# First chunk from turned tokens with late rates, and the last output columns kept in PSUM: a hybrid encoder layer on one Trainium2 core

## The chip, the cores and the metric

The kernel runs on one core of a Trainium2 chip. The metric is the device time of one execution in microseconds (us). The engines are PE (TensorE: products and transposes), DVE (VectorE), ACT (ScalarE), POOL (GpSimd) and SP (SyncE, which here only issues DMAs). PE writes into PSUM, eight banks of 512 float32 per partition; the others read it from there, POOL apart.

## The reference

One layer over 2048 tokens and 16 meta tokens ahead of them, 1024 channels, float32:

```python
u = rms_norm(h, pre_g)
proj = u @ w_in            # 1024 x 3584
glu_a, glu_b, conv_gate, q, k, v, sb_gate = split(proj)   # 512 columns each
c = glu_a * sigmoid(glu_b)
c = causal_depthwise_conv(c, conv_w, conv_b)              # width 31
c = silu(layer_norm(c, conv_ln_g, conv_ln_b))
c = (c @ w_pw2 + b_pw2) * silu(conv_gate)
s = stick_breaking_attention(heads(q), heads(k), heads(v)) * silu(sb_gate)  # 8 heads x 64
mixed = concatenate([c, s]) @ w_out                       # 1024 x 1024
return h + rms_norm(mixed, post_g)                        # meta tokens dropped
```

`rms_norm` divides a token's row by the root of its mean square (that factor is called its rate here) and multiplies by a gain per channel.

## The kernel before

Tokens are worked in four chunks of 512 (`TC`), each as four blocks of 128. A float32 product is made of three products of rounded parts: every operand is split into a high part (ACT rounds it) and a low part (DVE or POOL subtracts). So `uh` and `ul`, the two parts of the normed tokens, stand with channels on the partitions, eight pieces of 128 channels (`k`), with 16 + 512 columns; a group of 128 output columns of `w_in` takes 8 x 3 products of up to 512 columns (`mm3`, L571). In chunk 0, with the meta tokens, a group has two halves of 264 columns (`segs`, L593), 48 products in all. Weights come in slabs of 512 columns: the first time raw from `wpack` (two slabs a load, `load_raw`, L512, two buffers), split by ACT and POOL into four buffers `w`, and saved to `wscr` by POOL's queue if they are used again; later both parts come back from `wscr` in one load of 512 KB. `release` (L555) frees a slab and asks for the next.

The start: `load_in` (L631) loads the 512 tokens of chunk 0 as rows, `norm_in` (L641) squares them on ACT, makes the rate on POOL and scales them on DVE; `turn_in` (L659) turns them on PE, 32 transposes of 128 x 128, and ACT and DVE make `uh` and `ul` from PSUM with the gain `preg`. The meta tokens take the same way (`meta_norm`, `meta_in`). `in_proj` (L741) then runs the groups of chunk 0: G_B and G_A in turn for the four pieces `j` (sigmoid at the evacuation of G_B, product with it at that of G_A, into `ct`), then K, V and Q. The convolution of a piece is 31 taps on DVE over `ct[j]`, summing in the PSUM bank `cv`; its taps fill gaps of DVE.

Attention of a chunk runs per head and chunk of keys: scores on PE into a bank "T", sigmoid on ACT, a scan on DVE, transposes on PE, split on ACT and DVE, products with v into the bank "av". Products of the projections and of the output run between as filler, by a planner: `merge` (L1554) asks each stream when its next piece can start and keeps two streams in the proportion of `SHARES`; `when` and `in_us` put off steps (loads, splits) to the time at which the planner's clock thinks them ready. The instructions of each engine are in a fixed order once that is done. PSUM has two banks "mm", four "T", one "av", one "cv". SBUF tiles are rings by name: `ev` (six), `w` (four), `wr` (two), `pr` (nine).

The end: for the last chunk `out_part` (L1350) makes the output products of seven of the eight k in four steps of 256 columns (n). Three of them are copied from PSUM to `y` by ACT; the last one stays in two "mm" banks. Its second half is run to two pairs of k ahead (`AHEAD`), the rest in `out_last` (L1382), which then takes the four blocks of 128 tokens one after the other: the products of the last k, additions to `y`, squares on ACT, the product with `post_g` on POOL and DVE, the rate, and output = x + rate * y in two halves, each stored by SP.

In the trace nearly all instructions carry line 204, that of the helper which issues them, so rows are told apart by their tiles.

## Time and profile before

| | us |
|---|---|
| median of 3 runs (lowest to highest) | 1373.24 (1370.44 to 1373.45) |
| the profiled execution | 1371.76 |
| its span, first to last instruction | 1370.0 |
| PE busy in the span | 1312.5 (96%) |
| PE weight loads, beside the products | 1125.2 (82%) |
| DVE busy | 1006.8 (73%) |
| ACT busy | 732.0 (53%) |
| POOL busy | 657.0 (48%) |
| mean granted TensorE clock | 0.992 of full |

The engines work side by side, so their busy times don't add up. The profiled execution's time holds the span and 1.76 us around it. A product's duration in the timeline holds its way through the array, so a run of them is read by start to start, or by a group's span over its count.

### The profile page before, as it was taken

The numbers are of one execution on the slowest core, as the hardware profiler recorded it, in microseconds if no ns is written. First come the engines' busy times: TensorE is split into PE (matmuls) and PEld (weight loads), VectorE is DVE, ScalarE is ACT, GpSimd is POOL, SyncE is SP. The second block draws the span as 40 slices with busy tenths as digits, with TensorE's granted clock in tenths as the row PEclk, the third lists the DMA queues.
The fourth block names the chain that finished last, engine by engine and source line by source line (L and its number), as shares of the span: only waits on it lengthen the run. The fifth ranks groups of instructions, "written<-read, shape, count | busy, mean of one in ns | idle before, by whom it ended". The sixth has DMA issues, their size and how long they took to land. (4 is left out here: it accounts for less than half of the span.)

```text
span 1370.0 us, 21785 instructions
## 1 busy us (share of the span) xinstructions
PE 1312.5 (96%) x7599; PEld 1125.2 (82%) x7599; DVE 1006.8 (73%) x1402; ACT 732.0 (53%) x1452; POOL 657.0 (48%) x794
## 2 busy tenths in 40 slices
PE   6999988999998999999999999999999999999895
PEld 5998877887788977887789988888777898888794
DVE  3999663998984467984495477885549988898666
ACT  5233554444446544476655456578676576655443
POOL 5445486668356631387831243278786111222303
PEclk9999999999999999999999999999999999999998
DMA  4266978999975994686866696567677456587431
GB/s 142 94 164 197 345 233 248 302 316 320 348 245 179 319 339 145 202 236 204 264 223 185 191 326 198 173 190 235 201 220 241 147 173 174 173 276 237 159 109 62
DMA packets 160157, 299.12 MB, mean 218 GB/s; under 512 B 15392, under 2 KB 69344, under 8 KB 160048
## 3 DMA queue, kind: packets, MB, share of 16 engines
q1 hardware_dynamic: 145744, 247.65, 58.9%
q0 software_dynamic: 14304, 50.08, 9.4%
q8 instruction: 60, 0.98, 0.3%
q14 instruction: 49, 0.40, 0.1%
HBM read 216.02 MB, written 81.66 MB: 217 GB/s over the span
## 5 line engine op out<-in xcount | busy, mean ns | idle before, releaser
L204 PE MATMUL mm<-uh,w 128*128 128x512 f32 (+1 forms) x1728 | 522.9, 367 | 2.6 <-POOL w L204 1.5
L204 PEld LDWEIGHTS mm<-uh,w 128*128 128x128 f32 x1728 | 307.6, 188 | 51.5 <-POOL w L204 2.5
L204 DVE TENSOR_TENSOR al<-T,ah 128x512 fp32r<-128x512 f32 (+3 forms) x323 | 194.4, 602 | 168.9 <-ACT ah L204 167.9
L204 PE MATMUL mm<-ul,w 128*128 128x512 f32 (+1 forms) x864 | 312.0, 361 | 0.0
L204 DVE TENSOR_TENSOR_SCAN pr<-T,pr,zcol 128x512 f32<-128x512 f32 x192 | 245.1, 1277 | 55.5 <-ACT T L204 51.4
L204 ACT ACTIVATE ah<-T 128x512 fp32r<-128x512 f32 (+3 forms) x323 | 171.7, 532 | 164.7 <-PE T L204 159.5
L204 DVE SCALAR_TENSOR_TENSOR cv<-ct,cp,cv 128x512 f32<-128x512 f32 x319 | 239.4, 751 | 7.5
L204 ACT ACTIVATE T<-T 128x512 f32<-128x512 f32 (+2 forms) x320 | 167.6, 525 | 96.6 <-PE T L204 92.7
L204 POOL TENSOR_TENSOR acc<-acc,pd 128x512 f32<-128x512 f32 x150 | 193.8, 1292 | 50.6 <-ACT pd L204 43.7
L204 PE MATMUL T<-kk,q 128*128 128x512 f32 (+2 forms) x640 | 195.3, 388 | 2.9 <-DVE pr L204 1.7
L204 POOL TENSOR_TENSOR w<-wr,w 128x512 fp32r<-128x512 f32 x116 | 149.7, 1296 | 98.5 <-ACT w L204 95.2
L204 PE MATMUL T<-ident,pr 128*128 128x128 f32 x1088 | 173.2, 275 | 9.8 <-DVE al L204 6.5
L204 PEld LDWEIGHTS mm<-ul,w 128*128 128x128 f32 x864 | 162.7, 188 | 20.3 <-DVE ul L204 0.2
L204 PEld LDWEIGHTS T<-ident,pr 128*128 128x128 f32 x1088 | 134.1, 141 | 42.3 <-DVE al L204 8.2
L204 DVE TENSOR_TENSOR_SCAN pr<-T,tri 128x128 f32<-128x128 f32 (+3 forms) x128 | 103.8, 815 | 43.0 <-ACT T L204 42.5
L204 ACT ACTIVATE w<-wr 128x512 fp32r<-128x512 f32 x116 | 72.3, 628 | 104.8 <-DMA wr<-wpack 34.9
L204 PEld LDWEIGHTS T<-kk,q 128*128 128x128 f32 x640 | 106.1, 190 | 19.1 <-DVE pr L204 2.8
L204 PE MATMUL av<-ah,vk 128*128 128x512 f32 (+1 forms) x320 | 117.0, 366 | 1.4 <-ACT ev L204 1.4
L204 PE MATMUL av<-al,vk 128*128 128x512 f32 (+1 forms) x320 | 117.4, 367 | 0.0
L204 PE MATMUL mm<-uh,wr 128*128 128x512 f32 x320 | 115.0, 401 | 0.0
L204 ACT ACTIVATE pd<-ct,cp 128x512 f32<-128x512 f32 x150 | 105.9, 717 | 15.3 <-POOL acc L204 14.7
L204 POOL COPY cm<-pr 128x1 f32<-128x1 f32 x120 | 23.3, 206 | 153.4 <-DVE pr L204 153.2
(154 smaller groups left out, 1768.3 us busy)
## 6 DMA issues: line engine op xcount, KB each, us to landing
w<-wscr SPq DMA_DIRECT2D x125, 512.0 KB, 4.2
wscr<-w POOLq DMA_DIRECT2D x76, 512.0 KB, 5.8
wr<-wscr SPq DMA_DIRECT2D x59, 512.0 KB, 4.3
wr<-wpack SPq DMA_DIRECT2D x58, 512.0 KB, 5.2
kk<-kscr SPq DMA_DIRECT2D x80, 256.0 KB, 5.2
vk<-vscr SPq DMA_DIRECT2D x80, 256.0 KB, 4.1
q<-qscr SPq DMA_DIRECT2D x64, 256.0 KB, 6.8
tok<-x SPq DMA_DIRECT2D x16, 512.0 KB, 7.6
```

The source lines that it names most:

```text
L204: return call(out, *args, **kw)
```

## The change

The host gives a second copy of the first chunk with channels first (`xturn`: 16 meta tokens and 512 tokens). The kernel loads it in eight pieces, makes `uh` and `ul` straight from them with the gain but without the rates, and runs the first four groups (G_B and G_A of j = 0 and 1) on that. The token rows are loaded too, behind the turned pieces; their squares give the rates, which five transposes spread over the partitions into `row`. The evacuations of the four groups wait for `row`: G_B's sum is multiplied by it before the sigmoid, and the sigmoid once more after it, so that G_A's sum needs no product of its own. The turned pieces are then scaled and `uh` and `ul` are made again for the groups that follow. The first group does both its halves k by k; the second and third go into "T" banks. Twenty transposes of the identity stand ahead of everything on PE. The `ev` ring goes from six to five tiles. Raw weights are asked for one load at a time, when the planner thinks a buffer free. In `merge`, put-off steps that are ready sooner run first when no stream is ready; some bookkeeping of the planner is finer.

At the end the last 512 output columns instead of the last 256 stay in PSUM, in the banks "cv", "mm", "mm" and "T"; their weights are loaded once for each half of the tokens. The second half's products but two pairs of k are left to `out_last`. There the work is ordered anew: first 512 columns on DVE from "T" banks, last 512 straight from PSUM, the product with `post_g` and all outputs on DVE.

The diff, cut to its core:

```diff
-EV, WB, RAWS, PR, EHL = 6, 4, 2, 9, 4
+EV, WB, RAWS, PR, EHL = 5, 4, 2, 9, 4
-    [(29.8, 172.7)], [(73.1, 217.8)], [(116.0, 217.8)], [(125.1, 97.4), (160.4, 136.0)],
+    [(29.8, 172.7)], [(73.1, 217.8)], [(116.0, 217.8)], [(125.1, 97.4), (160.4, 126.3)],
...
+            else:
+                for n in (*range(0, D, OC), *range(D // 2, D, OC)):
+                    yield w_out, n, OC, 0, KD - 1
...
-                    in_us(2.0, load_raw)
+                    when(
+                        lambda: load_raw(min(RAWS, len(raws) + 1)), [], date=pe.now + 2.0, tag="wr")
...
+    def load_first_in():
+        uh, ul = u_now
+        load_raw(1)
+        sp.dma_start(cp, cpack)
+        keep["turned", 0] = 0
+        ts = []
+        for k in range(KD):
+            ts.append(T("pr", [P, TC], PR))
+            sp.dma_start(ts[k], xturn[:, k, NM:])
+            when(lambda k=k: part_in(0, k, ts[k], uh, ul), [ts[k], cp])
+            if k == 0:
+                mt = T("pr", [P, KD, NM], PR)
+                sp.dma_start(mt, xturn[:, :, :NM])
...
+        load_raw()
+        todo = []
+        for i in range(NTB // 2):
+            t = tok()
+            for b in range(2):
+                tb = 2 * i + b
+                sp.dma_start(t[:, b], x[tb * P : (tb + 1) * P, :])
+                todo.append((t[:, b], tb))
...
+        def spread():
+            pt = PT("cv", [P, TC])
+            for tb in range(NTB):
+                pe.transpose(
+                    pt[:, tb * P : (tb + 1) * P], rate0[:, tb : tb + 1].to_broadcast([P, P]),
+                    ident,
+                )
...
+            act.activation(row[:, NM:], pt, AF.Copy)
...
+            for go in waiting:
+                go()
+            for k in range(KD):
+                when(lambda k=k: times(k, pt), [ts[k], pt], [ts[k]])
...
+        def again():
+            yield need(given=lambda: len(scaled) == KD and "first" in keep)
+            keep["turned", 0] = 0
+            keep["normed"] = True
+            meta_in()
+            for k in range(KD):
+                when(lambda k=k: part_in(0, k, ts[k], uh, ul), [ts[k]])
+        return again()
+
+    def warm():
+        pt = PT("T", [P, TC])
+        for _ in range(20):
+            pe.transpose(pt[:, :P], ident, ident)
...
+        first = G_B, G_A, G_B + 1, G_A + 1
+        if c == 0 and g == first[-1]:
+            yield need(given=lambda: "row" in keep)
+        if c == 0 and g not in first:
+            keep["first"] = True
+            yield need(given=lambda: "normed" in keep)
...
+                def go():
+                    dve.tensor_tensor(t, pt, row[:, o : o + n], op=ALU.mult)
+                    act.activation(t, t, AF.Sigmoid)
+                    if j < 2:
+                        pool.tensor_tensor(t, t, row[:, o : o + n], op=ALU.mult)
+                if c == 0 and j < 2:
+                    with_rates(go)
...
+        def late(i, tags):
+            for e in range(2):
+                w = weights(w_out, D // 2 + e * OC, OC, 0, KD - 1)
+                keep["o", i, e] = yield from out_products(
+                    w, mix, range(KD - 1), i, False, tag=tags[e], free=True
+                )
+        yield from late(0, ("cv", "mm"))
+        keep["rest"] = late(1, ("mm", "T"))
...
+        def add_first(tb, a):
+            yt = y[tb // 2][:, tb % 2, 0:TC]
+            dve.tensor_tensor(yt, yt, a, op=ALU.add)
+            square(tb, yt, 0)
+            dve.tensor_tensor(yt, yt, pg[:, 0], op=ALU.mult)
+        def add_second(tb):
+            yt = y[tb // 2][:, tb % 2, TC:]
+            for e in range(2):
+                o, cols = keep["o", tb // 2, e][:, tb % 2], slice(e * OC, (e + 1) * OC)
+                square(tb, o, 1 + e)
+                dve.tensor_tensor(yt[:, cols], o, pg[:, 1, cols], op=ALU.mult)
...
+        rest = keep["rest"]
+        for _ in range(3):
+            next(rest)
+        a = [first(0)]
+        second(0)
+        a += [first(tb) for tb in range(1, NTB)]
+        add_first(0, a[0])
+        finish_off(rest)
+        second(1)
+        add_second(0)
+        add_first(1, a[1])
+        rate(0)
+        add_second(1)
+        add_first(2, a[2])
+        rate(1)
+        give_out(0)
+        add_first(3, a[3])
+        give_out(1)
+        add_second(2)
+        rate(2)
+        add_second(3)
+        rate(3)
+        give_out(2)
+        give_out(3)
...
-        load_in(0, 0)
-        load_in(0, 1)
-        m = load_meta()
-        load_raw()
+        warm()
+        once_more = load_first_in()
+        prepare()
         clear()
...
-        spent = [merge(iter(()), either(in_proj(0), either(turn_in(0), meta_in(m))), iter(()), [(1, 1)])]
+        spent = [merge(iter(()), either(in_proj(0), once_more), iter(()), [(1, 1)])]
...
+        "xturn": np.ascontiguousarray(
+            np.concatenate([f["meta_tokens"], f["x"][0, :TC]])
+            .reshape(NM + TC, KD, P).transpose(2, 1, 0)
+        ),
```

## Rows read from the trace of the kernel before

**Rows 1.** windows, four stretches; columns: busy us (instructions) per engine, granted clock, DMA share, GB/s:

```profile
0.00:42.90 42.90, 30.81 (x231) 28.83 (x232) 20.92 (x32) 21.09 (x36) 21.19 (x39) 1.00 0.43 138
42.90:1342.00 1299.10, 1270.03 (x7287) 1085.55 (x7287) 966.14 (x1333) 702.22 (x1386) 625.42 (x746) 1.00 0.71 224
1342.00:1353.70 11.70, 11.64 (x85) 10.81 (x83) 7.22 (x18) 4.72 (x17) 2.39 (x3) 1.00 0.01 1
1353.70:1370.00 16.30, 0.00 (x0) 0.00 (x0) 12.55 (x21) 3.94 (x14) 7.99 (x8) 0.60 0.34 129
```

**Rows 2.** waits of PE, first 60 us: us in total, times, longest:

```profile
PE T L204 <- DVE tok L204: 11.1, 4, 7.3
```

**Rows 3.** timeline of the start: start us, us, engine, operation, idle before and its releaser:

```profile
9.59 1.06 ACT L204 ACTIVATE ev<-tok 128x1024 bf16<-128x1024 f32 x1 [0.83 <-DMA tok<-x]
...
12.49 2.64 PEld L204 LDWEIGHTS T<-ident,tok 128*128 128x128 f32 x13 [1.80 <-DVE tok L204]
...
18.50 0.86 PEld L204 LDWEIGHTS T<-ident,tok 128*128 128x128 f32 x8 [0.24 <-DVE ul L204]
...
19.36 0.37 PE L204 MATMUL mm<-uh,w 128*128 128x264 f32 x1
...
19.60 2.72 DVE L204 SCALAR_TENSOR_TENSOR ul<-T,cp,uh 128x512 fp32r<-128x512 f32 x4 [0.19 <-ACT uh L204]
```

**Rows 4.** timeline of DVE, 26 to 235 us:

```profile
31.74 0.43 DVE L204 TENSOR_TENSOR ct<-mm,ehl 128x264 f32<-128x264 f32 x1 [2.48 <-PE mm L204]
...
43.42 0.43 DVE L204 TENSOR_TENSOR ct<-mm,ehl 128x264 f32<-128x264 f32 x1
...
143.25 0.75 DVE L204 SCALAR_TENSOR_TENSOR acc<-ct,cp,cv 128x512 f32<-128x512 f32 x1
```

**Rows 5.** DMA queues, 0 to 40 us: GB/s in slices of 1 us:

```profile
GB/s 0 25 266 373 410 389 406 354 276 388 350 51 0 0 0 0 0 20 211 287 70 348 113 0 16 0 0 0 0 123 350 51 0 0 29 264 231 0 0 16
```

**Rows 6.** DMA queues, 102 to 106 us, around the loads of km:

```profile
DMA packets 1660, 0.65 MB, mean 162 GB/s; under 512 B 1143, under 2 KB 1624, under 8 KB 1659
```

**Rows 7.** timeline of the end:

```profile
1341.71 0.39 PE L204 MATMUL av<-al,vk 128*128 128x512 f32 x1
...
1342.64 3.04 PE L204 MATMUL mm<-w,mixc 128*128 128x256 f32 x24
...
1345.53 2.32 PE L204 MATMUL mm<-w,mixs 128*128 128x256 f32 x18
1345.89 0.43 DVE L204 TENSOR_TENSOR mixs<-uh,mixs 128x256 fp32r<-128x256 f32 x1 [0.54 <-ACT mixs L204]
...
1352.31 0.63 ACT L204 ACTIVATE ev<-tok 128x512 bf16<-128x512 f32 x1 [1.16 <-DVE tok L204]
...
1352.33 1.32 PE L204 MATMUL T<-acc,mixs 128*128 128x512 f32 x6
...
1364.23 2.73 DVE L204 SCALAR_TENSOR_TENSOR ul<-tok,st,ul 128x512 f32<-128x512 f32 x4
```

**Rows 8.** groups by shape, 1342 to 1370 us: busy us, mean ns, idle before:

```profile
L204 DVE TENSOR_TENSOR tok<-tok,uh 128x256 f32<-128x256 f32 x4 | 4.8, 1204 | 1.3 <-ACT ev L204 1.3
...
L204 DVE TENSOR_TENSOR tok<-tok,T 128x512 f32<-128x512 f32 x4 | 2.7, 678 | 2.3 <-PE T L204 2.3
...
L204 DVE TENSOR_TENSOR tok<-mm,uh 128x256 f32<-128x256 f32 x4 | 1.7, 419 | 0.1
...
L204 DVE TENSOR_TENSOR uh<-uh 128x256 f32<-128x256 f32 x2 | 0.8, 422 | 0.0
...
L204 DVE TENSOR_REDUCE ss<-sq 128x1 f32<-128x3 f32 x4 | 0.6, 143 | 0.0
```

**Rows 9.** windows, 205 to 215 us:

```profile
205.00:215.00 10.00, 5.17 (x29) 4.27 (x29) 1.81 (x4) 2.65 (x7) 1.94 (x2) 0.93 0.73 211
```

**Rows 10.** timeline of ACT, 150 to 225 us:

```profile
212.35 1.15 ACT L204 ACTIVATE w<-wr 128x512 fp32r<-128x512 f32 x2 [7.80 <-DMA wr<-wpack]
```

**Rows 11.** DMA issues: count, KB each, median us to landing:

```profile
w<-wscr SPq DMA_DIRECT2D x125, 512.0 KB, 4.2
```

More of the change, by code (lines that the diff above doesn't have):

```diff
@@ L47 @@
 EARLY = 6
-AHEAD = 2
 LAG = 3
@@ L261, in run @@
             soon.remove(e)
+            here, clock.here = clock.here, e.n
             e.what()
+            clock.here = here
     def force(mark):
-        for e in clock.writers(mark):
-            run(e)
+        while clock.writers(mark):
+            run(clock.writers(mark)[0])
     def when(what, ins, outs=(), engine=None, date=0.0, tag=None):
@@ L628, in tok, with with_rates @@
+    waiting = []
+    def with_rates(go):
+        if "row" in keep:
+            go()
+        else:
+            waiting.append(go)
     def tok():
@@ L1290, in meta_keys @@
             fetch(js[0])
-        yield need(bm, tag="T")
+        yield need(bm, tag="T", given=None if part else room_for_turned)
         hold.remove(bm.name)
@@ L1321, in meta_keys, with out_products @@
             mixs[j] = hi, lo
-    def out_products(w, mix, ks, half, whole=True, bank=None, there=None):
+        hold.remove(ah.name)
+    def out_products(w, mix, ks, half, whole=True, bank=None, there=None, tag="mm", free=None):
         fresh = bank is None
@@ L1573, in merge @@
                     continue
+            early = [e for e in soon if e.at() < s.at()] if s.at() > pe.now + LEAD else ()
+            if early:
+                run(min(early, key=lambda e: e.at()))
+                continue
             s.go()
```

297 lines of the change are left out of this document (151 added, 146 removed).

## The prediction

> **What bounds the kernel now.** I read the windows first, cut where the change cuts [rows 1]. TensorE (PE) idles 12.1 us before 42.9 us, 29.1 us in the 1299.1 us up to 1342, 0.06 us from 1342 to 1353.7, and all of the last 16.3 us. So PE is the bound wherever the pipeline runs, and 28 of its 57.5 idle us sit at the two ends, where the change works. The waits say what the start is: PE waits 11.1 us for VectorE (DVE) to scale the tokens [rows 2]. The timeline shows the chain [rows 3]: loads, square sum on ScalarE (ACT), rate on GpSimd (POOL), scaling on DVE, transposes, split; the first product starts at 19.36 us. The timeline of the end [rows 7] shows PE with nothing but products up to 1353.65 and then a DVE chain, block by block, to 1366.96; the last store ends with the span at 1370.0, that is 16.35 us after PE.
>
> **Start: what goes and what comes.** Before, the four groups whose place changes (two of G_B, two of G_A) run back to back from 19.36; the last evacuations of the second and of the fourth start at 31.74 and 43.42 [rows 4], so a group costs (43.42-31.74)/2 = 5.84 us and the fourth ends near 43.2.
>
> After, SyncE (SP) issues one weight load (524 KB), the constants (76 KB), the turned tokens (8 x 262 KB) with the turned meta tokens (66 KB) between, another weight load, and only then the 2.1 MB of plain tokens. The last turned piece has 2.76 MB up to and with it. Summing the bytes per us of the first stretch [rows 5], 2.76 MB are through at 9.7 us. Loads share the engines with what is queued behind them: the fourth token load, 2.1 MB deep, is 7.7 us by that sum, but ACT, free before, starts on it at 9.59 [rows 3], so 1.9 us come on top. The meta piece is 1024 runs of 64 bytes. The nearest row is the 4 us around the loads of km: 1143 packets under 512 B, and 0.65 MB moved [rows 6] where the 380 GB/s of the first stretch would have moved 1.5; that is at most 2.3 us lost. I bound the cost by 0 and 2.3 and take 1. Last piece: 9.7+1.9+1 = 12.6. Then ACT's high part (0.63 for 512 columns [rows 7]), DVE's low part (2.72/4 = 0.68 [rows 3]) and six products at 5.84/48 = 0.12: the first group ends at 14.6. It takes a new piece each 0.75 to 0.9 us, about what DVE needs for one and PE for its six products, so PE follows the loads.
>
> The Trainium skill ("DMA: Bandwidth & Descriptors", Specifications) asks for 512 B per descriptor for line rate. By [rows 6] the small runs do cost engine time out of proportion to their bytes; by the page alone nothing more can be priced, and by the row at its upper bound the first group ends 1 us later.
>
> Second group: its weights are the load behind the turned pieces, which lands near 13.5; ACT and POOL split it while the first group ends; I take 0.5 us of wait. Third and fourth: their weights come behind the plain tokens, 5.2 MB deep, at 17 to 19 us, before the third group at 20.9. The rates need the last tokens (about 16), one square (1.06 [rows 3]), POOL's power, five transposes and two copies: near 20, before the fourth group, whose banks and evacuations wait for them, starts at 26.8. So the fourth group ends at 14.6+0.5+3 x 5.84 = 32.6, against 43.2: **-10.6 us**. The 32 transposes that go lie before 19.36 and are in this number; the first 13 stood at 0.20 us a weight load and the last eight at 0.107 [rows 3]: the lower and the higher of the clock levels, after idle time and after steady work. The 20 warming transposes run from about 2 to 6 us while the loads are under way, and cost nothing.
>
> What the change adds is a second making of uh and ul from scaled tokens, between the fourth group and the fifth. It can't be early: it overwrites what the fourth group reads, and it is emitted after that group's last evacuation, so on DVE it stands behind 0.43 us of that evacuation [rows 4], then about as much for the meta columns, then 8 x 0.68. With 0.2 for the hand-over the eighth is ready 6.5 us after the fourth group's end. The fifth group's first half wants all eight in 8 x 0.36 = 2.9 us. Nothing else is there for PE. With the last products behind it that is a stall of **+4 us** (bounds: 1 if DVE gets ahead of the evacuation, 7 if convolution taps of 0.75 us slip between). Scaling itself (8 x 0.68 on DVE) falls to 20-26 us, before any tap can start, beside PE's groups, and costs PE nothing; it holds the bank "cv", so the convolution starts near 26 instead of 32.2 [rows 4]. Start in all: **-6.6 us**, bounds -9 and -2.
>
> The Trainium skill ("TensorE: Matmul & The Clock Gate", HAM oscillation) warns that waits for loads between short bursts of products throw the clock back to its lower level. In this trace the weight loads at 12.49 show that level after 1 to 2 us gaps in sparse work [rows 3]. Were the first group to run at it, six products would take 1.3 us, not 0.7, and it would end 3 to 4 us later; the start's bounds hold that too.
>
> **Middle.** PE's idle 29.1 us [rows 1] are mostly waits for weights: between 205 and 215 us PE works 5.2 of 10 us, and the granted clock falls to 0.93 after it has stood [rows 9], behind an ACT that waited 7.8 us for a raw weight load [rows 10]. All this is tied to PE's position and moves with it. Three things are less sure. The convolution's sums of chunk 0 end at 144.0 [rows 4]; DVE starts them 6 us earlier but has 6.5 us more to do in between, so they end at the same time while PE is 6 us earlier: conv_norm stands 6 us later in PE's order. What needs it (the pointwise projection) came long after, so I take +0.5, bounds 0 and +6. The ev ring has five tiles instead of six, weights are asked for one load at a time and deferred steps run sooner: each can move these stalls either way. I take 0, bounds -8 and +8: a quarter of the idle time each way.
>
> **End.** PE's work is the same number of products, since deferring a product keeps it. What stays after attention's last product is 84 products of 256 columns and the last k's 5.7 us, against 48 before (24 and 18 in [rows 7], with six more), so attention ends 36 x 0.12 = 4.3 us earlier and PE about when it did. Count from attention's last product: 24 products to 2.9 us (1342.64 to 1345.53 [rows 7]); they cover most of the last head's gating (1342.1 to 1346.3 [rows 7]; its first half, which first(0) needs, I put at 3.1); first(0) 3.1-3.8, second(0) to 5.2, first(1..3) to 7.3, 60 products to 14.5, second(1) to 15.9. DVE starts at 4.0. A first half is an add 0.68, a wait for ACT's square (0.63 [rows 7], 0.8 with its read and the hand-overs), and a product by post_g of 512 columns: the 256-column one takes 1.20 while POOL works and 0.42 without [rows 7, 8]; POOL has only the powers left, so 0.68. That is 2.15 x 4. A second half is 2 x 0.42 x 4 from PSUM, the four sums 4 x 0.14 [rows 8], the eight outputs at 0.68 (2.73/4 [rows 7]) 5.4. Together 8.6+3.4+0.6+5.4 = 18.0, so DVE ends at 22.0 and the last store 3.04 later (1370.0-1366.96), at 25.0. PE ended at 15.9, so the tail is 9.1 against 16.35: **-7.2 us**. Bounds: if only what follows second(1) counted, the tail would be 7.9 (-8.5); if attention without its filler ran 4 us slower, -3.
>
> The second 512 columns' weights are loaded twice: seven more slabs of 512 KB at most. A slab then feeds 12 products, 1.44 us, and lands 4.2 us after issue [rows 11]. With four to six in flight this is covered, and DMA is nearly idle there, 0.01 [rows 1].
>
> **Sum.** -6.6+0.5-7.2 = -13.3 us. The profiled execution took 1371.76 (span 1370.0 and 1.76 around it); the median of the runs is 1373.24, 1.5 above. From the median: about 1360.
>
> **The rivals.**
> A. The start is given back: where weights are saved and loaded, 140 to 215 us, loading sets the time, and an earlier PE only waits longer there. For it: the 7.8 us wait [rows 10]. Against: those loads are asked for by PE's progress and so move too. 1373.2-7.2+0.5 = 1366.5.
> B. The re-laid schedule also closes the stall at 205-215 and its like: one load asked for at a time no longer blocks SP. For it: that stall is one late load [rows 10]. Against: nothing else of that stretch changed. A further -8: 1352.
> C. Slower: weight slabs at the end. When the slab for each 1.44 us of products is asked for only as the one before is freed, each costs 4.2-1.44 = 2.8 us. It turns the whole change slower from six slabs on (5 x 2.8 = 14); ten of the 14 would give 1360+28 = 1388. For it: attention's k and v loads sit in the same queue. Against: six buffers.
> D. It doesn't do what it says: the rates or second making hold PE so long (stall over 10 us), and attention, latency-bound without filler, eats the end's gain: 1373.2+0.8-3 = 1371.
>
> **Chances.** Forecast (1355-1364) 0.58, A 0.14, B 0.13, C 0.07, D 0.08. About 0.2%, 2.7 us, is what can be told from no change here. Faster takes the forecast, A and B: 0.85; same, most of D: 0.07; slower, C and the rest of D: 0.08. The range 1351 to 1369 takes in B, A and the start's and end's bounds.
>
> **What would show it.** First product before 8 us; the first group's pace by DMA; the fourth group's end at 31-35; a PE wait of 3-5 us for ul right after; the wait for tok gone; the convolution's last sum near 144 still; PE's last product some 9 us before the span's end, with DVE products by post_g at 0.7 per 512. Wrong if PE waits for w in the last 40 us, if the stall after group four is near zero or above 8, or if the middle's idle time leaves 21-37 us.

## The result: 1359.1 us, and the profile after

The changed kernel took 1359.09 us (median of 4 runs, 1356.11 to 1360.08) against 1372.21 of the kernel before on the same chip (4 runs, 1370.44 to 1373.45): a ratio of 0.9902, 95% interval 0.9885 to 0.992, that is 13.1 us saved. The profiled execution took 1360.08 with a span of 1357.9. The forecast was 1360.0, a saving of 13.3. The total came out, its parts did not: the start saved little or nothing, the end more than forecast, and the rest of the change, forecast at half a microsecond lost, saved some 2 to 4 us, a part of it by the loading of raw weights. That the sum came within a microsecond is luck: its errors cancel.

The windows of the kernel after, cut as before [rows 1] (busy us and instructions of PE, PE's weight loads, DVE, ACT, POOL; granted clock, DMA share, GB/s):

```profile
0.00:42.90 42.90, 33.97 (x217) 32.50 (x217) 21.64 (x36) 23.29 (x42) 23.09 (x37) 0.88 0.54 189
42.90:1342.00 1299.10, 1278.96 (x7306) 1093.88 (x7307) 971.10 (x1360) 711.26 (x1405) 624.31 (x746) 0.99 0.70 227
1342.00:1349.50 7.50, 7.49 (x64) 7.29 (x62) 5.80 (x13) 2.35 (x9) 1.56 (x2) 1.00 0.19 72
1349.50:1357.90 8.40, 0.00 (x0) 0.00 (x0) 4.87 (x11) 1.31 (x6) 1.54 (x2) 0.64 0.50 187
```

Read PE's instruction counts beside its busy time. Up to 42.9 us PE is busy 3.2 us longer than before, and has issued 217 recorded instructions instead of 231 (before, 32 token transposes were among them; after, 20 warming and five spreading ones). The granted clock there is 0.88 instead of 1.00: PE is busier because its products are slower. The tail without PE is 8.4 us instead of 16.3.

The start of the kernel after, PE's timeline (start, us, engine, operation, count; idle before and what ended it):

```profile
1.82 4.53 PE L203 MATMUL T<-ident 128*128 128x128 f32 x20 [1.82 <-POOL ident masks.py:199]
8.61 0.39 PE L203 MATMUL mm<-uh,w 128*128 128x264 f32 x1 [2.26 <-ACT uh L203]
...
12.53 0.42 PE L203 MATMUL mm<-ul,w 128*128 128x264 f32 x1
12.75 0.64 PE L203 MATMUL mm<-uh,w 128*128 128x264 f32 x2
13.19 0.42 PE L203 MATMUL mm<-ul,w 128*128 128x264 f32 x1
...
15.99 0.28 PE L203 MATMUL mm<-ul,w 128*128 128x264 f32 x1
16.11 0.41 PE L203 MATMUL mm<-uh,w 128*128 128x264 f32 x2
16.36 0.28 PE L203 MATMUL mm<-ul,w 128*128 128x264 f32 x1
...
22.45 0.60 PE L203 MATMUL cv<-ident,rate 128*128 128x128 f32 x4
...
28.43 0.81 PE L203 MATMUL T<-uh,w 128*128 128x264 f32 x2 [3.17 <-POOL w L203]
...
42.91 0.39 PE L203 MATMUL mm<-uh,w 128*128 128x264 f32 x1 [1.61 <-ACT uh L203]
44.26 0.40 PE L203 MATMUL mm<-ul,w 128*128 128x264 f32 x1 [0.96 <-DVE ul L203]
```

From 12.53 to 13.19 three products take 0.66 us; from 15.99 to 16.36 they take 0.37. Those are the lower and the higher of the clock levels (1.2 and 2.4 GHz). The windows of the same stretch show when PE ran at which:

```profile
10.00:15.00 5.00, 4.99 (x28) 4.99 (x29) 3.93 (x6) 4.81 (x8) 1.49 (x1) 0.66 1.04 407
15.00:20.00 5.00, 5.00 (x43) 5.00 (x42) 0.00 (x0) 4.29 (x9) 1.33 (x2) 1.00 1.01 351
...
25.00:30.00 5.00, 1.83 (x10) 1.61 (x9) 3.25 (x6) 0.93 (x3) 4.29 (x5) 0.74 0.08 22
30.00:35.00 5.00, 5.00 (x27) 5.00 (x27) 3.64 (x7) 0.95 (x2) 1.65 (x2) 0.57 0.54 188
```

The clock falls after each of the idle gaps (2.26, 3.17 us), and a stretch at full busy then issues 27 or 28 products instead of 43. The wait for `w` in the third group has its cause on two other engines, ACT first and then POOL:

```profile
23.25 0.58 ACT L203 ACTIVATE row<-cv 128x512 f32<-128x512 f32 x1
...
23.92 1.28 ACT L203 ACT_TABLE_LOAD   x1
25.21 0.73 ACT L203 ACTIVATE ehl<-ehl 128x264 f32<-128x264 f32 x2
```

```profile
25.71 1.44 POOL L203 TENSOR_TENSOR ehl<-ehl,row 128x264 f32<-128x264 f32 x2 [2.24 <-ACT ehl L203]
27.11 3.80 POOL L203 TENSOR_TENSOR w<-wr,w 128x512 fp32r<-128x512 f32 x3
```

POOL works in order. Its products of the sigmoid with `row` wait for ACT, ACT's sigmoid waits for its table, and the split of the next weight slab stands behind those products. The table load holds ACT from 23.92 to 25.20. And `row` itself came late: ACT started on the last block of tokens at 18.31, when it had landed (forecast: about 16), POOL's power of the rates ended at 22.2, and ACT wrote `row` from 23.25 on, where the forecast had the rates near 20. DVE then shows the end of the fourth group and the second making:

```profile
41.49 0.42 DVE L203 TENSOR_TENSOR ct<-mm,ehl 128x264 f32<-128x264 f32 x1
...
43.46 5.38 DVE L203 SCALAR_TENSOR_TENSOR ul<-pr,cp,uh 128x512 fp32r<-128x512 f32 x8
48.77 7.07 DVE L203 SCALAR_TENSOR_TENSOR cv<-ct,cp,cv 128x512 f32<-128x512 f32 x9
55.75 0.42 DVE L203 TENSOR_TENSOR ct<-mm,ehl 128x264 f32<-128x264 f32 x1
```

The last evacuation of the fourth group is at 41.49, against 43.42 before [rows 4], but the first of the sixth group is at 55.75, against 52.34.

The end of the kernel after, timeline:

```profile
1329.96 0.39 PE L203 MATMUL av<-al,vk 128*128 128x512 f32 x1
...
1338.99 0.69 DVE L203 TENSOR_TENSOR tok<-tok,uh 128x512 f32<-128x512 f32 x1 [0.79 <-ACT ev L203]
...
1348.62 0.88 PE L203 MATMUL T<-acc,mixs 128*128 128x256 f32 x6
...
1351.78 2.73 DVE L203 SCALAR_TENSOR_TENSOR ul<-tok,st,ul 128x512 f32<-128x512 f32 x4
```

The product with `post_g` (`tok<-tok,uh`) takes 0.69 us for 512 columns, where 256 columns took 1.20 beside a working POOL before [rows 8]. PE ends at 1349.50 and DVE 5.0 us later.

To follow a gain through the kernel I read four points in each profiled execution, by DVE rows that every kernel has: the first evacuation of a K group of chunk 0 (K), the first `ct` of chunk 1 (ct1), the first `mixc<-mm` sum of chunk 1 (co1) and of the last chunk (co3).

| kernel | K | ct1 | co1 | co3 | span | span - co3 | median |
|---|---|---|---|---|---|---|---|
| before | 70.0 | 241.4 | 501.8 | 1247.4 | 1370.0 | 122.6 | 1372.2 |
| after | 73.3 | 241.8 | 500.9 | 1247.2 | 1357.9 | 110.7 | 1359.1 |
| old_start | 73.9 | 237.7 | 498.4 | 1245.8 | 1357.2 | 111.4 | 1359.9 |
| split_now | 72.5 | 235.8 | 496.1 | 1242.6 | 1353.2 | 110.6 | 1357.4 |
| old_end | 72.0 | 239.8 | 500.0 | 1246.1 | 1367.1 | 121.0 | 1368.8 |
| new_start | 68.3 | 237.2 | 499.7 | 1244.9 | 1356.0 | 111.1 | 1358.7 |
| both_undone | 74.1 | 239.0 | 500.8 | 1246.8 | 1366.4 | 119.6 | 1368.8 |
| late_start | 71.7 | 239.3 | 499.6 | 1245.9 | 1356.8 | 110.9 | 1360.1 |
| conv_on_pool | 69.4 | 236.6 | 498.2 | 1243.1 | 1356.4 | 113.3 | 1356.1 |
| start_and_split | 69.0 | 240.2 | 500.9 | 1246.5 | 1358.3 | 111.8 | 1359.4 |
| early_x | 73.9 | 236.5 | 496.9 | 1246.0 | 1358.6 | 112.6 | 1359.1 |
| raw_as_before | 79.7 | 241.3 | 504.0 | 1250.6 | 1361.5 | 110.9 | 1362.8 |
| all_together | 69.6 | 234.8 | 496.5 | 1244.0 | 1355.4 | 111.4 | 1355.5 |
| raw_alone | 70.3 | 236.1 | 500.8 | 1247.8 | 1371.0 | 123.2 | 1367.0 |

The last column but one is the clearest reading of the whole study: 110.6 to 113.3 us wherever the new end is in, 119.6 to 123.2 wherever it isn't. The first column says little about the later ones.

How far single executions scatter can be read here too. In the ten kernels with the new end the instructions of every engine stand in one and the same order from 240 us on (in raw_as_before only from some 520 us on), for the planner comes back to the same order there. Yet from ct1 to the end of the span the other nine take 1116.1 to 1122.1 us. So an edit of the start can act on the time only by moving ct1, and a difference of a few microseconds between two single traces, at ct1 or behind it, shows nothing by itself; the medians decide.

### The profile page after: what moved, and what is told of

Read it like the earlier page. It is cut to its first block, busy times and chain, and to the rows that moved or that the text cites. A ratio compares the mean times of both kernels' runs of the same rounds, so it can differ in the third digit from the quotient of the medians.

```text
span 1357.9 us, 21813 instructions
## 1 busy us (share of the span) xinstructions
PE 1320.4 (97%) x7584; PEld 1133.7 (83%) x7584; DVE 1003.4 (74%) x1417; ACT 738.2 (54%) x1459; POOL 650.5 (48%) x786
## 4 chain that ended last, share of the span: by engine, by line
PE 80%; DVE 7%; DMA 4%; ACT 3%; issue 3%; POOL 2%; SPq 0%; DVEq 0%; POOLq 0%; ACTq 0%
PE mm L203 51%; PE T L203 20%; PE av L203 8%; DVE cv L203 2%; DMA tok<-x 1%; DVE pr L203 1%; ACT ev L203 1%; DMA wr<-wpack 1%; POOL w L203 1%; DVE tok L203 1%; DVE ul L203 1%; DVE al L203 1%; POOL ev L203 1%; DVE acc L203 1%; DMA wscr<-w 1%
## 5 line engine op out<-in xcount | busy, mean ns | idle before, releaser
L203 PEld LDWEIGHTS mm<-uh,w 128*128 128x128 f32 x1664 | 302.2, 191 | 52.6 <-ACT uh L203 4.5
L203 PE MATMUL mm<-ul,w 128*128 128x512 f32 (+1 forms) x832 | 307.0, 369 | 1.1 <-DVE ul L203 1.0
L203 ACT ACTIVATE T<-T 128x512 f32<-128x512 f32 (+2 forms) x320 | 167.4, 525 | 110.7 <-PE T L203 108.0
L203 PEld LDWEIGHTS mm<-ul,w 128*128 128x128 f32 x832 | 158.6, 191 | 22.3 <-DVE ul L203 1.7
L203 POOL COPY cm<-pr 128x1 f32<-128x1 f32 x120 | 23.7, 200 | 146.7 <-DVE pr L203 145.8
```

What stands on the lines that cost most here:

```text
L203: return call(out, *args, **kw)
```

## The experiments

Each ran in five rounds beside the kernel before; ratios are to that kernel, with 95% intervals.

**old_start: the start of before put back.**

```diff
-        warm()
-        once_more = load_first_in()
-        prepare()
+        load_in(0, 0)
+        load_in(0, 1)
+        m = load_meta()
+        load_raw()
 ...
-        spent = [merge(iter(()), either(in_proj(0), once_more), iter(()), [(1, 1)])]
+        meta_norm(m)
+        prepare()
+        spent = [merge(iter(()), either(in_proj(0), either(turn_in(0), meta_in(m))), iter(()), [(1, 1)])]
```

> The changed kernel with only its start undone: the first chunk's tokens are loaded as rows, scaled and turned as before, and no group waits for the rates; everything else is as changed (ev ring of five, one raw load at a time, late split of the last weights, new end). In the changed kernel's trace the first K evacuation on DVE starts at 73.3 us, before the change at 70.0: the start as built runs 3.3 us late, not 6.6 early. Theory 1 (the start buys nothing, its lateness is taken up by later waits): first K evacuation back at 70, time 1357 to 1360. Theory 2 (the lateness is carried to the end): 1355.8. Rival, the forecast's reading (the start is worth 6.6): 1365.7.

Measured: 1359.93 us (1358.78 to 1361.28), ratio 0.9917 (0.9904 to 0.9929). The new start is worth 0.8 us by the medians against the kernel after and 2.6 against split_now, which ran beside it and is the same program (see there); the intervals overlap both times. But K came at 73.9, not near 70: under the changed planner the old start is itself late, so this run compares two equally late starts and does not yet show that a start in time would be worth nothing. Why it is late is a row of DVE and one of POOL. DVE and POOL of old_start:

```profile
12.85 5.43 DVE L203 TENSOR_SCALAR q<-q,st 16x1024 f32<-16x1024 f32 x1 [0.70 <-POOL st L203]
```

```profile
12.79 4.94 POOL L203 TENSOR_TENSOR w<-wr,w 128x512 fp32r<-128x512 f32 x4
```

and the same two of before:

```profile
13.14 0.74 DVE L204 TENSOR_SCALAR q<-q,st 16x1024 f32<-16x1024 f32 x1 [0.70 <-POOL st L204]
```

```profile
14.29 4.97 POOL L204 TENSOR_TENSOR w<-wr,w 128x512 fp32r<-128x512 f32 x4 [1.18 <-ACT w L204]
```

In old_start POOL's splits begin 0.06 us ahead of DVE's scaling, and DVE ends 0.55 us after the last of them; in before they begin after it, and the same instruction takes 0.74. Which of two instructions that share no data begins first makes 4.7 us for DVE here. It came again in both_undone, which has the same start (5.42 us, 0.05 behind POOL's). PE then waits 3.75 us for `ul`, where it waited 0.99 before.

**split_now: the last weights split at once, as before.**

```diff
-            in_us(
-                6.0 + i, lambda raw=raw, hi=hi, lo=lo: split(raw, hi, lo), [raw], [hi, lo]
-            )
+            split(raw, hi, lo)
```

> The changed kernel with one line undone: the last k's output weights of the last chunk are split at once when their loads are issued, not 6 and 7 us later. Theory (ACT then waits in order for the load of these weights, the splits and sigmoids of attention stand behind it, PE idles and its clock falls near 1270 to 1290, as before the change): PE busy in 1270-1290 falls from 17.9 to about 16, granted clock there to about 0.83, time 1359.1+4.7 = 1363.8. Rival (that stretch changed because the order around it did): 1358.5 to 1360.

Measured: 1357.36 us (1355.32 to 1358.06), ratio 0.9895 (0.9882 to 0.9908): no loss, so the late split is not what changed the stretch of 1270 to 1290 us. Compared row by row, its instructions stand on every engine in the very order of the kernel after; the edit changes nothing in the order of the work. The run is therefore a second sample of the kernel after, and shows how far two samples lie apart: 1.7 us in the medians, and in the profiled executions 6.0 us at ct1. Two windows each, around PE's wait for a rate of POOL in the attention of chunk 0 (2.99 us in after, 3.21 in split_now); the kernel after:

```profile
170.00:175.00 5.00, 1.81 (x13) 1.23 (x11) 3.62 (x6) 3.40 (x8) 2.46 (x5) 0.92 1.09 349
175.00:180.00 5.00, 4.68 (x12) 3.71 (x13) 2.25 (x4) 0.62 (x1) 4.81 (x9) 0.50 0.99 266
```

and split_now, 1 us earlier in its execution:

```profile
169.00:174.00 5.00, 1.96 (x14) 1.37 (x12) 3.71 (x6) 3.08 (x7) 2.35 (x4) 1.00 1.08 341
174.00:179.00 5.00, 4.77 (x22) 3.98 (x23) 3.17 (x6) 1.92 (x4) 4.75 (x9) 1.00 0.87 233
```

The same program, nearly the same idle time of PE: in one execution the granted clock then falls to 0.50, and 12 products run where 22 run in the other.

**old_end: the end of before put back** (`out_part`, `out_last`, the order of the last slabs and the last corner of `SHARES`).

```diff
-            if c + 1 < NCH:
-                yield from proj_specs(c + 1)
-            else:
-                for n in (*range(0, D, OC), *range(D // 2, D, OC)):
-                    yield w_out, n, OC, 0, KD - 1
+            yield from proj_specs(c + 1) if c + 1 < NCH else out_specs(0, KD - 1)
 ...
-        for n in range(0, D // 2, OC):
+        for n in range(0, D, OC):
```

> The changed kernel with only its end undone: 256 columns stay in PSUM, the second half's rest is two pairs, post_g on POOL and DVE, blocks one after the other; the weights of the last 512 columns are loaded once. Theory (the tail after PE's last product is 16.4 us so, 8.4 as changed, and PE's work is the same): 1359.1+8.0 = 1367.1. Rival (attention, with more filler left beside it, ends later or earlier by some us): 1363 to 1371 with PE's last product moved; a tail below 14 us would refute the theory.

Measured: 1368.8 us (1365.86 to 1372.04, 12 runs), ratio 0.9974 (0.996 to 0.9989): the new end is worth 9.7 us by the medians. The windows of old_end, cut at PE's last product:

```profile
1246.13:1350.26 104.13, 101.31 (x678) 91.08 (x676) 70.13 (x112) 48.30 (x101) 20.19 (x21) 0.98 0.44 141
1350.26:1367.10 16.84, 0.00 (x1) 0.00 (x0) 12.62 (x21) 4.07 (x14) 8.08 (x8) 0.59 0.33 125
```

Its tail is 16.84 us against 8.40 after: 8.4 us of the gain lie there. PE's stretch before is 1.8 us longer than after (104.13 against 102.28, from 1247.22 to 1349.50), but with the new end the same stretch takes 102.1 to 104.8 us in the ten kernels, so that part is not clear of the scatter.

**new_start: the start mended.** The products with `row` go from POOL to DVE, the second making comes in two halves of 264 columns, each right after the fourth group's half, and 38 warming transposes stand ahead.

```diff
-                        pool.tensor_tensor(t, t, row[:, o : o + n], op=ALU.mult)
+                        dve.tensor_tensor(t, t, row[:, o : o + n], op=ALU.mult)
 ...
-        for _ in range(20):
+        for _ in range(38):
 ...
-            yield need(given=lambda: len(scaled) == KD and "first" in keep)
+            if c == 0 and g == first[-1]:
+                yield need(given=lambda: len(keep["scaled"]) == KD)
+                keep["remake"](*part[0])
```

> The changed kernel with its start mended in three places: the sigmoid's second product with the rates on DVE instead of POOL (the third group's second weight slab stands behind it on POOL, PE waits 3.2 us); uh and ul made again in two halves, each as soon as the fourth group's half is through (PE waited 1.6+1.0 us and then ran at DVE's pace); 38 warming transposes instead of 20 (PE idled 2.3 us ahead of the first product and the granted clock fell). The clock stood at 0.66, 0.74, 0.57 and 0.71 in four slices of 5 us. Both theories: first K evacuation near 64 us, PE idle up to 60 us down from 9.9 by 5 or more. Theory 1 (what the start wins is lost in waits of the next 400 us, which go by DMA and DVE): 1357 to 1359.5. Theory 2 (carried to the end): 1350 to 1352.

Measured: 1358.7 us (1357.74 to 1359.43), ratio 0.9907 (0.9894 to 0.992). K came at 68.3, 5.1 us sooner than after: the mending worked, though short of the 64 expected. The time did not follow. A place where a lead can go is seen in DVE's and PE's timelines; new_start:

```profile
197.38 7.04 DVE L203 TENSOR_TENSOR acc<-acc,ev 128x512 f32<-128x512 f32 x4
...
204.94 0.41 DVE L203 TENSOR_TENSOR al<-T,ah 128x256 fp32r<-128x256 f32 x1
```

```profile
205.41 0.47 PE L203 MATMUL T<-ident,pr 128*128 128x128 f32 x1 [5.21 <-DVE al L203]
```

Four additions of the convolution's norm stand ahead of `al` on DVE, at 1.76 us each while POOL splits weights, and PE has nothing else to do: 5.2 us, as much as K had gained. That this wait took the lead is not shown: conv_on_pool removes it, and ct1 stays. The mended start also moved something else, which the expectation did not name: on DVE the norm of chunk 0's convolution starts at 179.1 us here, at 161.5 in the kernel after, at 150.8 in old_start and at 146.7 before.

**late_start: 75 warming transposes instead of 20.**

```diff
-        for _ in range(20):
+        for _ in range(75):
```

> The changed kernel with 75 warming transposes ahead of the first product instead of 20. At 0.11 to 0.21 us each the first product comes 6 to 11 us later than 8.6; the loads are by then all there, so part of it is caught up, and the first evacuation of K should come 2 to 8 us later than 73.3. Theory 1 (the stretch from 140 to 220 us sets its own end, whatever the start does): the first sum of conv_out stays within 213 to 218 us, and the time within 1.5 us of 1359. Rival (the start counts one for one, and the mended start lost its gain by another accident of the order): conv_out's first sum and the time come later by as much as K does, 1361 to 1367.

Measured: 1360.06 us (1358.0 to 1362.2), ratio 0.9921 (0.9908 to 0.9935). Not a later start but an earlier one: although the first product waits until 12.84, K comes at 71.7. From that product to 40 us PE runs at the higher clock (1.00 in each window of 5 us), and it waits 0.85 us for weights, where the kernel after waits 3.17. Behind the waits for the second making the clock falls as in the kernel after (0.62 from 40 to 45 us). So this run can't tell what a delay costs; the time is that of after within the intervals.

**conv_on_pool: the mended start, and the fourth piece of chunk 0's convolution on POOL.**

```diff
-APART = (), (), (2, 3), (1, 2, 3)
+APART = (3,), (), (2, 3), (1, 2, 3)
```

> The mended start (row products on DVE, second making in two halves, 38 warming transposes: 1358.7) with the fourth piece of the first chunk's convolution on POOL instead of DVE: 31 taps of 0.75 us, some 23 us, taken from DVE where it is busy 18 to 19.5 of 20 us (40 to 160 us). Theory DVE (DVE's convolution sets when the first chunk's pointwise products can start, and swallows what the start gains): the sums end well before 178 and the first sum of conv_out comes at 211 or sooner (216.2 with the mended start), the time falls by 3 to 8 us to 1351 to 1356. Theory DMA (the transfers from 140 to 180 us, DMA share 1.0, swallow it): conv_out's first sum stays at 214 to 218, and the time at 1358.7 within 2 us, or worse where POOL's taps of about 1.3 us stand ahead of its weight splits.

Measured: 1356.05 us (1355.06 to 1358.26), ratio 0.9895 (0.9881 to 0.9909). The convolution's norm starts at 167.9 instead of 179.1 and the first sum of `conv_out` comes at 210.8, as theory DVE had it, and the 5.2 us wait of PE is gone (3.5 us at most, for `mixc`). Yet ct1 is at 236.6, 0.6 us sooner than in new_start, and the time 2.7 us less, not 3 to 8; the intervals overlap. DVE's load is a part of it at most. The norm is still later than in the kernel after (161.5) and before (146.7): a start that has both K and the convolution in time was not run.

**both_undone: the change without its start and its end.** The edits of old_start and old_end together.

```diff
-        once_more = load_first_in()
+        load_in(0, 0)
+        load_in(0, 1)
 ...
-    [(29.8, 172.7)], [(73.1, 217.8)], [(116.0, 217.8)], [(125.1, 97.4), (160.4, 126.3)],
+    [(29.8, 172.7)], [(73.1, 217.8)], [(116.0, 217.8)], [(125.1, 97.4), (160.4, 136.0)],
```

> The changed kernel with the start and the end of the kernel before: what is left is the ev ring of five, raw weights asked for one load at a time and the planner's finer bookkeeping. Undoing the end alone gave 1368.8, undoing the start alone 0.8 us. Theory (three parts that add up, the rest of the change is worth some 3 us): 1369.6, faster than before by 1.5 to 4 us, with PE busy about 86 of the 100 us from 1260 on. Rival (what is left is worth nothing by itself, the 3 us come from the two new ends together): 1372, within 1 us of before.

Measured: 1368.81 us (1366.82 to 1371.93), ratio 0.9986 (0.9977 to 0.9996): 1.9 us faster than before (0.5 to 3.2). The parts add up: with old_start the end is worth 0.9986 - 0.9917, that is 9.5 us, as in old_end.

**start_and_split: the mended start with the late split undone**, on new_start:

```diff
-            in_us(
-                6.0 + i, lambda raw=raw, hi=hi, lo=lo: split(raw, hi, lo), [raw], [hi, lo]
-            )
+            split(raw, hi, lo)
```

> The mended start together with the last weights split at once as in the kernel before: the best of each so far (1358.7 and 1357.36). If what each gave is real and adds up, 1357.0 and never above 1358.5; if both were only scatter of the order of work in the middle, anywhere from 1357 to 1361. Predicted by both theories of the start: K's first evacuation near 68, conv_out's first sum at 211 to 217.

Measured: 1359.41 us (1356.37 to 1363.28), ratio 0.9914 (0.9897 to 0.9932). By the order of its instructions this is new_start again. Taken together, the ten runs of the mended start have a median of 1358.97, the eight of the kernel after and split_now one of 1357.94. The profiled executions agree: K at 68.7 on the mean of the two mended ones against 72.9, and ct1 at 238.7 against 238.8. The 4.3 us are gone by then, and nothing is gained that these runs can show.

**early_x: chunk 1's tokens loaded early.**

```diff
+        for half in range(2):
+            in_us(30.0 + 12 * half, lambda half=half: load_in(1, half))
         spent = [merge(iter(()), either(in_proj(0), once_more), iter(()), [(1, 1)])]
-        for half in range(2):
-            in_us(4.0 + 6 * half, lambda half=half: load_in(1, half))
```

> The changed kernel with the second chunk's token loads (2.1 MB) and what follows them on ACT, POOL and DVE asked for 30 and 42 us into the kernel, where the DMA share is 0.2 to 0.4, instead of near 150, where it is 1.0. Theory DMA (the transfers of 140 to 180 us set the end of the stretch): 2.1 of the 13.6 MB moved there go, at 340 to 400 GB/s that is 5 to 6 us; the share falls below 1.0 over part of 140 to 180, the first ct of the second chunk comes 3 to 6 us sooner than 241.8, and the time falls to 1354 to 1356. Theory order (the stretch is held by the order of PE, DVE and POOL around attention without filler, not by bytes): DMA share falls just as well, but the first ct of the second chunk stays within 238 to 243, and the time within 1.5 us of 1359.

Measured: 1359.08 us (1356.93 to 1360.36), ratio 0.9905 (0.9886 to 0.9924). The windows of the kernel after, then of early_x:

```profile
140.00:160.00 20.00, 19.87 (x99) 15.89 (x97) 17.68 (x26) 8.92 (x19) 11.44 (x19) 1.00 1.00 352
160.00:180.00 20.00, 16.49 (x75) 13.20 (x73) 12.40 (x23) 8.07 (x16) 13.57 (x26) 0.86 1.04 327
```

```profile
140.00:160.00 20.00, 19.92 (x93) 15.90 (x92) 17.86 (x27) 8.74 (x18) 11.75 (x19) 1.00 1.01 334
160.00:180.00 20.00, 18.57 (x99) 15.24 (x98) 15.55 (x28) 5.39 (x12) 12.29 (x22) 1.00 0.90 312
```

The DMA share of 160 to 180 falls from 1.04 to 0.90. The time stays. ct1 is at 236.5, 5 us sooner than in the profiled execution of after, but split_now, the same program as after, has 235.8. So taking these loads out of the stretch gains nothing. It does not clear the transfers altogether: 2.1 MB went, but by the GB/s of the windows the bytes moved from 140 to 180 fell by 0.7 MB alone (13.6 to 12.9), and up to 160 the engines are as full as before.

**raw_as_before: raw weights asked for as before.**

```diff
-                    when(
-                        lambda: load_raw(min(RAWS, len(raws) + 1)), [], date=pe.now + 2.0, tag="wr")
+                    in_us(2.0, load_raw)
```

> The changed kernel with raw weight loads asked for as before (up to two at once, 2 us on) instead of one at a time when a buffer is thought free. The change without its start and its end is still worth 0.14% (1.9 us, 0.6 to 3.2). Theory (that is the raw loads): 1361 and a wait of several us of ACT for a raw load comes back in 200 to 215 or in 1270 to 1290 us. Rival (it is the rest of the planner, or scatter): 1359 within 1.3 us, with no such wait.

Measured: 1362.81 us (1358.66 to 1365.32), ratio 0.993 (0.9907 to 0.9954): 3.7 us more than after by the medians, intervals overlapping. Not by a wait of several us for a raw load (ACT's longest between 60 and 290 us is 3.1). The first product came at 17.05, after 11.5 us of waiting for ACT's `uh`, and K at 79.7; yet ct1 is at 241.3, as in the kernel after. Between ct1 and co1 it loses 3 us against the kernel after (262.7 against 259.1), but new_start takes 262.5 there and raw_alone 264.7, so the place of the loss is open. The half of the expectation that named the wait failed; the loss may as well come of the start, which this edit delays by 8 us. raw_alone, below, has the raw loads without the new start.

**all_together: the edits of early_x and split_now on conv_on_pool.**

```diff
+            in_us(30.0 + 12 * half, lambda half=half: load_in(1, half))
 ...
-            in_us(4.0 + 6 * half, lambda half=half: load_in(1, half))
 ...
-                6.0 + i, lambda raw=raw, hi=hi, lo=lo: split(raw, hi, lo), [raw], [hi, lo]
+            split(raw, hi, lo)
```

> Mended start, fourth piece of the first chunk's convolution on POOL, second chunk's tokens early, last weights split at once. Theory DMA and DVE together: the second chunk's first ct at 228 to 234 (236.6 with the convolution on POOL alone), time 1350 to 1353. Theory order: second chunk's first ct at 235 to 242, time 1355 to 1359.

Measured: 1355.45 us (1353.98 to 1357.22), ratio 0.988 (0.9859 to 0.99). The lowest of all, 16.8 us under before, and 3.6 under after, from which its interval can't quite be told apart. ct1 is at 234.8: what the theories of DMA and DVE together had wanted (228 to 234) did not come, what the theory of order had (235 to 242) did by a hair.

**raw_alone: the kernel before with the raw loads asked for one at a time**, and nothing else.

```diff
-                    in_us(2.0, load_raw)
+                    when(
+                        lambda: load_raw(min(RAWS, len(raws) + 1)), [], date=pe.now + 2.0, tag="wr")
```

> The kernel before with one part of the change alone: raw weights asked for one load at a time, when a buffer is thought free. Putting that part back into the changed kernel cost 3.7 us (1362.81 against 1359.09), and all of the change but its start and its end was worth 1.9. Theory (raw loads carry what the two ends don't): 1368 to 1370.5 against 1372, with the 7.8 us wait of ACT for a raw load at 212 gone. Rival (the loss when it was put back came of the laid-out order around the new start, K's first evacuation being at 79.65 there, and the loads by themselves are worth nothing): 1371 to 1373.

Measured: 1367.01 us (1364.59 to 1372.79, 12 runs), ratio 0.9973 (0.9957 to 0.9989): 3.7 us saved (1.5 to 5.9) by this part alone. The order of its instructions differs from before's only from 173 to 475 us, so the gain has to come from there. Its profiled execution was the longest of the twelve and can't show the gain in the time, but it shows what went. ACT's waits from 60 to 290 us (total, times, longest), before and raw_alone:

```profile
ACT w L204 <- DMA wr<-wpack: 20.6, 5, 7.8
```

```profile
ACT w L204 <- DMA wr<-wpack: 7.6, 3, 4.6
```

The 7.8 us wait [rows 10] is gone. Behind it on ACT stood the `ah` that DVE needs for `al`, and PE stood waiting for that `al`. This is the longest of PE's waits from 140 to 300 us in before; the longest in raw_alone is 1.0:

```profile
PE T L204 <- DVE al L204: 4.8, 1, 4.8
```

ct1 comes at 236.1 instead of 241.4, with K in the same place (70.3 and 70.0), though two executions of one program can lie as far apart; at co1 this execution is 1.0 us ahead, at co3 0.4 behind.

The raw loads are not all of the middle. Windows from 1270 to 1290 us of before, raw_alone and both_undone:

```profile
1270.00:1290.00 20.00, 15.99 (x85) 12.87 (x84) 16.61 (x26) 9.88 (x20) 9.22 (x9) 0.83 0.38 128
```

```profile
1270.00:1290.00 20.00, 15.64 (x80) 12.66 (x80) 16.81 (x27) 9.78 (x20) 9.24 (x9) 0.83 0.39 136
```

```profile
1270.00:1290.00 20.00, 16.98 (x104) 13.76 (x103) 17.66 (x31) 11.72 (x23) 8.79 (x9) 1.00 0.55 168
```

In both_undone the clock stays up there and PE gets 104 products done instead of 85; in raw_alone it does not. From co3 to PE's end before and raw_alone take 106.3 and 106.9 us, both_undone and old_end, which have the old end too, 103.2 and 104.1. So a gain of some 2 to 3 us seems to lie here, in one execution of each kernel, and neither the raw loads nor the late split made it.

## Why the prediction was right in sum and wrong in its parts

**Start (-6.6 forecast; -0.8 by the medians, -2.1 by the ratios of old_start and after, neither clear of the scatter).** Two steps failed. First, the start itself did not come out: what follows the fourth group was forecast 6.6 us sooner, and the sixth group's first evacuation came 3.4 us later. Of the 8.7 us that the fourth group's end missed (41.3 against 32.6) the rows account for 7.8: first group 2.0 (end 16.60 against 14.6), because not the loads but the lower clock after the wait of 2.26 set its pace; no wait ahead of the second, -0.5; the five spreading transposes in PE's order 0.7 (22.45 to 23.13); the wait for `w` 3.2; and 2.4 for 24 products at 0.22 instead of 0.12 behind it. The prediction had the third group's weights at 17 to 19 us and asked only when they land, not who splits them and what stands ahead of the split on POOL. It should have: the change puts a product on POOL behind ACT's sigmoid. It also had the rates near 20, some 3 us too early, since the last tokens landed at 18.3 and not at 16.

The remaking, forecast at +4 of waiting, cost 1.61 + 0.96 of waiting, and again a lower clock behind it (0.71 from 45 to 50 us), which was not in the sum. The Trainium skill ("TensorE: Matmul & The Clock Gate", HAM oscillation) was quoted for that risk; the trace agrees with it twice in the first 35 us, after the waits of 2.26 and 3.17, and at 175 us in one execution of two. The forecast had priced the risk at 3 to 4 us, from its own rows, and left it to the bounds.

The second making had another price. The forecast let the convolution of chunk 0 start near 26 us and end near 144 all the same; it started at 35.8 and ended at 158.9 (before, at 32.2 and 144.0). What that costs was not isolated.

Second, the step "all this is tied to PE's position and moves with it" failed: it is what made a gain at the start count one for one. PE's busy time between K and ct1 is nearly the same in these kernels, while the stretch itself grows or shrinks. Windows from K to ct1, of new_start, split_now and raw_as_before:

```profile
68.28:237.22 168.94, 159.29 (x916) 137.13 (x915) 130.64 (x198) 78.83 (x157) 103.71 (x133) 0.98 0.75 248
```

```profile
72.51:235.75 163.24, 157.78 (x919) 136.01 (x918) 121.77 (x187) 78.77 (x157) 104.27 (x133) 1.00 0.77 253
```

```profile
79.65:241.33 161.68, 157.70 (x919) 135.90 (x918) 130.96 (x194) 78.31 (x157) 103.75 (x133) 1.00 0.78 255
```

PE needs some 158 us there at full clock. The earliest K has 9.7 us of idle time in the stretch, the latest 4.0: of 11.4 us between their K, 4.1 are left at ct1. These are single executions, but the medians say the same: ten runs of the mended start, with K 4.3 us sooner, are no faster than eight of the kernel after. This is rival A's outcome for the start. Its reason (loading sets the time) is not borne out, for moving 2.1 MB of loads away did not move the time, though the stretch filled up again (early_x). What holds the stretch differs from one laid-out order to the next: DVE additions ahead of `al` in new_start, a rate on POOL in the kernel after, the clock. That it would also swallow a gain much larger than 5 us, which order would pass it on, and what the later convolution has to do with it, stays open.

**Middle (+0.5 forecast, bounds -8 to +8; -1.9 by both_undone, -3.7 by raw_alone).** The likeliest value failed, the bound held. The reading under it was wrong as well: PE's 29.1 us of idle time are not mostly waits for weights. In the kernel before PE waits 6.7 us of them for `w`; 4.8 more, from 209 to 214, are the wait for `al` behind ACT's wait for a raw load, and most of the others are for DVE and POOL. Rival B named the mechanism, one load asked for at a time, with a price of 8; it was half of that at most, and came on top of rival A and not instead of it. What the planner's bookkeeping and the `ev` ring add was not taken apart; the windows from 1270 to 1290 hint that it isn't nothing. The late split, which the prediction doesn't mention, is nothing.

**End (-7.2 forecast; -9.5 to -9.7).** Right in its steps: the tail is 8.4 us (9.1 forecast), DVE works at 0.69 per 512 columns, PE never waits for a weight slab in the last 40 us (rival C), attention's last product starts 19.5 us before PE's end instead of 11.9 (15.9 forecast), and PE's end did not suffer. The gain is 2.3 to 2.5 us more than forecast. 0.7 of that is the tail's own. The rest would have to lie before PE's end, where the forecast had no change: 104.1 and 103.2 us from co3 to PE's last product with the old end (old_end, both_undone), 102.3 in the kernel after, but 102.1 to 104.8 over all kernels with the new end, so this part is not shown.

**Sum.** Taken one after the other by the ratios (before, both_undone, old_start, after) the parts are 1.9 for the middle, 9.5 for the end and 2.1 for the start, 13.5 together; by the medians before and after lie 13.1 apart. The forecast's start was about 5 us too good, and its middle and end together about 5 too bad; that they cancel is luck. Of its signs, the first product (8.61, before 8), the fourth group's end (41.3, 31 to 35), the stall after it (2.6, 3 to 5), the convolution's last sum (158.9, near 144) and the middle's idle time (20.1, 21 to 37) all missed, the last of which the prediction had itself named as a sign of being wrong; the wait for `tok` went, and the signs of the end came. Had the start been all there was, the forecast would have been wrong.

## What to carry to other kernels

Follow a gain past the next stretch in which the same engine waits for others, by matched rows, before counting it: a lead of 4 us at 70 us was gone by 240, while 8 us taken behind the last product stayed. For each wait that a change puts on an in-order engine, list what that engine does for someone else right behind it, here a weight split behind a product that waits for a table. And before crediting an edit that a planner digests, look whether the order of instructions changed at all: here two samples of one order lay 1.7 us apart in their medians.

## What the runs showed of the hardware that was not expected

- A DVE instruction on 16 partitions took 5.43 us instead of 0.74 because four POOL instructions on SBUF, back to back, had begun 0.06 us ahead of it; DVE got through only behind the last (old_start; again in both_undone, 5.42 us). The Trainium skill ("SBUF — State Buffer", SBUF: two separate sides) tells of a pair of ports that one of the two engines holds for a whole instruction, the other blocked; the rows agree that it is all or nothing, and here it lasted over four instructions. That the ports are the cause is the page's account; no run here tests it.
- With the same instructions in the same order, an idle spell of some 3 us in front of PE's products was followed by a granted clock of 0.50 in one execution and of 1.00 in another, and the positions at 240 us were 6 us apart.
- The granted clock of a profile's first microseconds does not fit the products here: it reads 1.00 from 0 to 10 us in the kernel after, while its 20 warming transposes stand 0.21 us apart. In late_start it reads 1.00 as well, and the same transposes stand 0.21 us apart up to 7.0 us and 0.11 from 7.2 us on.
